# The first phase of a hybrid streaming encoder step: its loads in packed rows, the samples ahead of the prompt, and its splits placed ahead of waits

## The chip, the cores and the metric

The kernel runs on one core of one Trainium2 chip. The time is the device time of one execution in microseconds. The kernel before took 1387.94 us, the median of three runs (1385.57 to 1388.15).

Engines are named as the profile names them: PE (TensorE, matrix products) and PEld (its weight loads), DVE (VectorE), ACT (ScalarE), POOL (GpSimd) and SP (SyncE, which issues most loads). SBUF is the on-chip memory that the engines read, PSUM the one that TensorE writes.

## The reference

One layer of a mixer network, for 256 new frames (the prompt) and 32 frames of a running stream (the samples), with the same weights and a width of 2048:

```python
mod = jax.nn.silu(c) @ ada_w + ada_b                      # c: one vector per request group; ada_w 2048 x 6144
shift, scale, gate = jnp.split(mod, 3, axis=-1)
h = rms_norm(x, g_pre) * (1.0 + scale[:, None]) + shift[:, None]
proj = h @ w_in                                           # w_in 2048 x 18432
gb, gc, gu, zc, q, k, v, zr, ma, mb = jnp.split(proj, SPLIT_POINTS, axis=-1)
y_conv = gb * causal_conv3(gc * gu) * jax.nn.silu(zc)     # short convolution with a carried history
y_ret = head_rms(retention(rope(q), rope(k), v)) * jax.nn.silu(zr)   # 8 heads, carried state
merged = jax.nn.sigmoid(ma) * (y_conv @ w_branch[0]) + jax.nn.sigmoid(mb) * (y_ret @ w_branch[1])
x = x + gate[:, None] * rms_norm(merged @ w_out, g_post)
```

All is float32. Besides the new x the step returns the convolution's history and the retention's state of both groups.

## The kernel before

All products have the 288 frames (256 of the prompt, 32 samples) as columns, and run over contraction tiles of 128 rows. Float32 products are made of three faster ones: each operand is split into a high part (the value rounded to the type `F32R`) and a low part (the value less its high part), and `hi*hi`, `hi*lo` and `lo*hi` are summed in PSUM. For a weight piece, ACT makes the high part `whi` (a cast) and DVE the low part `wlo` (a subtraction); for `h` they are `hh` (ACT) and `hl` (DVE).

The change lies in the first phase (lines 210 to 441), in which four engines' work is in the order written (`manual_schedule`): each engine does its instructions strictly in the order of the code, and waits at the first that isn't ready. The phase does this:

- It loads x in three tiles (two of 128 prompt frames, one of 32 samples) on SP's queue, and eight small loads on ACT's queue bring the vectors (c, ada_b, the convolution's state and weights, norm_pre) as rows of 128 into two tiles, `crows` and `vrows`, which TensorE turns into columns (lines 380 and 382).
- `square(t)` (ACT, line 386) sums the squares of tile t; `norm(t)` (POOL takes the power, DVE scales x, line 391) normalises it; `turn_x(t)` (TensorE, line 401) transposes it in 16 pieces of 128 columns, and ACT and DVE copy these out into `xT` (line 403).
- `modulate(i)` (line 296) multiplies silu(c) with one piece of ada_w, that is 512 rows of it and, of 256 output columns, both the shift and the scale. Four pieces make one group `g`: the modulation of two contraction tiles. `gather_mod(g)` (line 306) turns the result into columns, and `factors(g)` (lines 309 to 329) makes the multiplier and the addend of each row, then, on ACT, `h` and `hh`; `low_parts(g)` makes `hl` on DVE.
- `multiply(i)` (line 339) multiplies the group's two tiles of `h` with a piece of w_in: 256 rows by 1024 columns, of q, of k or of the first half of v. It does so in four steps j of two output tiles each, 12 products a step; after a step the sums are added to `firsts` in SBUF (line 363; in group 0 they are copied, line 361). Between the steps `cut()` splits half a weight piece ahead of its use: `usual` and `rare` (line 337) say after which steps.
- There are eight groups of four ada_w pieces and three w_in pieces. The list `loads` has them in order of use, and `load(i)` issues them on SP's queue. Each piece is 1 MB and takes one of nine buffers `raw`; a load waits until the piece that had its buffer is used. `modulate` of a group stands between the `multiply` calls of the group before.

At a group's end, in its third `multiply` and ahead of step 1, stand `gather_mod` and `factors` of the next group; `cut()` follows after step 1, `low_parts` after step 2:

```python
                if nxt and j == 1:
                    gather_mod(g + 1)
                    factors(g + 1)
```

The later phases (the remaining columns of w_in, the retention, both branches and the output product) load pieces of 256 columns and split them in the same way by `product` (line 163), whose products are lines 148, 149 and 151. They aren't edited.

Of the kernel before, what the change touches and what calls it, by code (L numbers as in the profile page):

```python
# [10 lines left out]
F32 = mybir.dt.float32  # L11
F32R = mybir.dt.float32r
AF = mybir.ActivationFunctionType
ALU = mybir.AluOpType
# [77 lines left out]

@with_exitstack
def hybrid_step(ctx: ExitStack, tc, x_prompt, x_sample, c_prompt, c_sample, state_conv, state_ret,
                ada_w, ada_b, norm_pre, norm_post, w_in, conv_w, conv_b, w_branch, w_out,
                rope_t, dec_t, kdec_t, qdec_t, blk,
# [113 lines left out]
    with ExitStack() as phase:  # L210
# [14 lines left out]
        x = []  # L225
        for src in (x_prompt[0, 0:P], x_prompt[0, P:TP], x_sample[0]):
            x.append(buffer("raw", KH * WC, F32, RAW, MORE_RAW))
            nc.sync.dma_start(out=x[-1][:src.shape[0]], in_=src)


        def rows(t, r, v, n):
            A.dma_start(out=t[r * NK:(r + n) * NK], in_=v.rearrange("(k p) -> k p", p=P))

        crows = st.tile([3 * NK, P], F32, name="crows")
        rows(crows, 0, c_prompt[0], 1)
        rows(crows, 1, c_sample[0], 1)
        rows(crows, 2, ada_b[0, D:2 * D], 1)
        vrows = st.tile([NR * NK, P], F32, name="vrows")
        rows(vrows, R_SC, state_conv[0, 0].rearrange("r d -> (r d)"), 2)
        rows(vrows, R_CW, conv_w[0].rearrange("r d -> (r d)"), 3)  # L240
        rows(vrows, R_CB, conv_b[0], 1)
        rows(vrows, R_GP, norm_pre[0], 1)
        rows(vrows, R_AB, ada_b[0, 0:D], 1)
# [11 lines left out]
        def load(i):  # L255
# [3 lines left out]
            raw = buffer("raw", KH * WC, F32, RAW, MORE_RAW)  # L259
            if is_mod:  # L260
                v = raws[i] = raw.rearrange("p (k s c) -> p k s c", k=MOD, s=2)
                for s in range(2):
                    c0 = s * D + g * GS * P
                    nc.sync.dma_start(out=v[:, :, s, :], in_=ada_w[0, u * MOD * P:(u + 1) * MOD * P, c0:c0 + GS * P]
                                      .rearrange("(k p) c -> p k c", p=P))
            else:
                v = raws[i] = raw.rearrange("p (k c) -> p k c", k=GS)
                n = 1 if g == 0 and u == 0 else GS
                for k in range(0, GS, n):
                    r0 = (g * GS + k) * P  # L270
                    nc.sync.dma_start(out=v[:, k:k + n], in_=w_in[0, r0:r0 + n * P, FIRST[u]:FIRST[u] + PIECE]
                                      .rearrange("(k p) c -> p k c", p=P))
# [533 lines left out]
```

## Time and profile before

| | before |
|---|---|
| median of 3 runs | 1387.94 us |
| the profiled execution | 1388.77 us |
| its span in the profile | 1387.0 us |
| PE busy | 1348.6 us (97%) |
| DVE, ACT busy | 840.1, 552.9 us |
| mean granted clock of TensorE | 0.987 |
| read from memory | 261.75 MB |
| mean rate of the loads | 193 GB/s |

The profile tells the busy time of each engine, for the span or for any stretch of it; the clock that the throttle granted to TensorE (1 is full speed); who waited for whom; and the chain of work that ended last. A row of instructions has start and length, engine, line of the code and operation, `out<-in`, shapes, and in brackets the idle time of the engine ahead of it with what ended it. "L386 firsts<-raw" is such a name: the square's output is thrown away into a tile that isn't used yet. A DMA issue (SPq, ACTq) has the time that issuing took; its landing is told apart. Matmuls overlap, so that busy PE time counts a stretch in which products follow one another as fully busy.

### The profile page before, as it was taken

To read this page: it belongs to the slowest core of one execution; us is meant where nothing else is said; L and a number is where in the kernel's file an instruction comes from. 1 tells how busy PE (TensorE), PEld (TensorE's weight loads), DVE (VectorE), ACT (ScalarE), POOL (GpSimd) and SP (SyncE) were. 2 spreads that over 40 slices of the span, in tenths; PEclk is the share of its full clock that TensorE was granted. 3 is DMA by queue.
4 is the path that set the end of the run, shared out by engine and by line. 5 is a ranking of instruction groups with operands and counts; after the bars stand their busy time and mean duration, and the time that the engine had idled before them with its cause. 6 is when DMAs were issued, how large, how long until landed. Compare 5 with 4: busy or idle time off the path is not lost.

```text
span 1387.0 us, 24180 instructions
## 1 busy us (share of the span) xinstructions
PE 1348.6 (97%) x10250; PEld 1309.0 (94%) x10250; DVE 840.1 (61%) x1394; ACT 552.9 (40%) x824; POOL 10.0 (1%) x18
## 2 busy tenths in 40 slices
PE   4999999999999999999999999999999999999996
PEld 3888889999999999999999999999999999999996
DVE  3476768965555866666777767775555334555443
ACT  3434325754444433333334333333333333334442
POOL 0000000000000000000000000000000000000000
PEclk8999999999999999999999999999999999999998
DMA  9988864544445567566666656665455455557431
GB/s 332 371 308 302 275 225 136 166 135 161 144 147 158 182 204 217 187 214 203 199 191 202 199 185 190 213 217 182 156 165 171 153 167 167 159 175 225 158 111 69
DMA packets 240740, 267.81 MB, mean 193 GB/s; under 512 B 5604, under 2 KB 233236, under 8 KB 240020
## 3 DMA queue, kind: packets, MB, share of 16 engines
q1 hardware_dynamic: 234336, 256.13, 56.2%
q10 hardware_dynamic: 6296, 10.13, 2.9%
q8 instruction: 80, 1.31, 0.4%
q14 instruction: 28, 0.23, 0.1%
HBM read 261.75 MB, written 4.49 MB: 192 GB/s over the span
## 4 chain that ended last, share of the span: by engine, by line
issue 67%; PE 27%; DVE 3%; ACT 2%; DMA 1%; POOL 0%; DVEq 0%; POOLq 0%; ACTq 0%
PE acc L148 4%; PE acc L151 4%; PE acc L149 4%; PE pair L355 3%; PE pair L354 3%; PE pair L358 3%; PE small L296 2%; ACT h L326 1%; DVE firsts L363 1%; PE aux L476 1%; DVE wlo L284 1%; PE pair L401 1%; ACT whi L283 1%; PE aux L477 1%; PE aux L478 1%
## 5 line engine op out<-in xcount | busy, mean ns | idle before, releaser
L114 DVE TENSOR_TENSOR wlo<-raw,whi 128x1024 fp32r<-128x1024 f32 x336 | 410.6, 1222 | 348.7 <-ACT whi L113 347.9
L113 ACT CAST whi<-raw 128x1024 fp32r<-128x1024 f32 x336 | 352.6, 1050 | 516.7 <-PE acc L149 486.6
L148 PE MATMUL acc<-hh,whi 128*128 128x288 f32 x1920 | 531.4, 299 | 1.0 <-DVE firsts L363 1.0
L149 PE MATMUL acc<-hl,whi 128*128 128x288 f32 x1920 | 530.4, 297 | 0.0
L148 PEld LDWEIGHTS acc<-hh,whi 128*128 128x128 f32 x1920 | 361.0, 188 | 5.1 <-issue 1.7
L149 PEld LDWEIGHTS acc<-hl,whi 128*128 128x128 f32 x1920 | 361.2, 188 | 0.3
L151 PE MATMUL acc<-hh,wlo 128*128 128x288 f32 x1920 | 330.0, 294 | 0.0
L151 PEld LDWEIGHTS acc<-hh,wlo 128*128 128x128 f32 x1920 | 283.1, 188 | 0.0
L355 PE MATMUL pair<-hl,whi 128*128 128x288 f32 x384 | 111.1, 304 | 4.8 <-DVE hl L334 4.8
L354 PE MATMUL pair<-hh,whi 128*128 128x288 f32 x384 | 112.6, 307 | 2.8 <-ACT hh L327 2.0
L620 DVE SCALAR_TENSOR_TENSOR gbc<-raw,sc,gbc 128x256 f32<-128x256 f32 x240 | 100.3, 477 | 13.3 <-DMA raw<-in_ada_w_dram 13.3
L363 DVE TENSOR_TENSOR firsts<-pair,firsts 128x576 f32<-128x576 f32 x84 | 63.3, 754 | 41.5 <-PE pair L358 41.5
L358 PE MATMUL pair<-hh,wlo 128*128 128x288 f32 x384 | 84.2, 300 | 1.1 <-DVE wlo L284 1.1
L354 PEld LDWEIGHTS pair<-hh,whi 128*128 128x128 f32 x384 | 73.9, 192 | 11.5 <-ACT whi L283 5.7
L355 PEld LDWEIGHTS pair<-hl,whi 128*128 128x128 f32 x384 | 74.1, 193 | 6.8 <-DVE hl L334 6.4
L149 PE MATMUL acc<-ml,whi 128*128 128x288 f32 x256 | 70.6, 297 | 0.0
L148 PE MATMUL acc<-mh,whi 128*128 128x288 f32 x256 | 70.2, 296 | 0.0
L148 PE MATMUL acc<-ch,whi 128*128 128x288 f32 x256 | 70.0, 296 | 0.0
L148 PE MATMUL acc<-yh,whi 128*128 128x288 f32 x256 | 69.9, 296 | 0.0
L149 PE MATMUL acc<-yl,whi 128*128 128x288 f32 x256 | 69.8, 295 | 0.0
L149 PE MATMUL acc<-cl,whi 128*128 128x288 f32 x256 | 69.5, 294 | 0.0
L284 DVE TENSOR_TENSOR wlo<-raw,whi 128x1024 fp32r<-128x1024 f32 x48 | 58.3, 1217 | 15.3 <-ACT whi L283 15.3
(179 smaller groups left out, 1333.8 us busy)
## 6 DMA issues: line engine op xcount, KB each, us to landing
raw<-in_w_in_dram SPq DMA_DIRECT2D x143, 1024.0 KB, 5.1
raw<-in_ada_w_dram SPq DMA_DIRECT2D x64, 512.0 KB, 7.3
raw<-in_w_branch_dram SPq DMA_DIRECT2D x32, 1024.0 KB, 5.6
raw<-in_ada_w_dram SPq DMA_DIRECT2D x16, 1024.0 KB, 5.1
raw<-in_w_out_dram SPq DMA_DIRECT2D x16, 1024.0 KB, 5.5
raw<-in_x_prompt_dram SPq DMA_DIRECT2D x2, 1024.0 KB, 6.1
out_dram<-ns SPq DMA_DIRECT2D x16, 128.0 KB, 5.3
x<-in_x_prompt_dram ACTq DMA_DIRECT2D x1, 2048.0 KB, 8.0
```

Source lines behind the costliest of these rows:

```text
L113: A.copy(out=hi, in_=src)
L114: V.tensor_tensor(out=lo, in0=src, in1=hi.bitcast(F32), op=ALU.subtract)
L148: nc.tensor.matmul(ps, hi[:, k, fs], xh[:, k0 + k, :], start=first and k == 0, stop=False)
L149: nc.tensor.matmul(ps, hi[:, k, fs], xl[:, k0 + k, :], start=False, stop=False)
L151: nc.tensor.matmul(ps, lo[:, k, fs], xh[:, k0 + k, :], start=False, stop=last and k == n - 1)
L284: V.tensor_tensor(out=lo, in0=raws[i][:, k], in1=hi.bitcast(F32), op=ALU.subtract)
L296: nc.tensor.matmul(pm[at:at + 32, :GS * P], cs[:, kt, :], v[:, k, s, :], start=kt < 2, stop=kt >= NK - 2, tile_position=(0, at))
L354: nc.tensor.matmul(ps, hi[:, fs], hh[:, kt, :], start=k == 0, stop=False)
L355: nc.tensor.matmul(ps, hi[:, fs], hl[:, kt, :], start=False, stop=False)
L358: nc.tensor.matmul(ps, lo[:, fs], hh[:, kt, :], start=False, stop=k == GS - 1)
L363: V.tensor_tensor(out=sums, in0=pp[:, :, :T], in1=sums, op=ALU.add)
L620: V.scalar_tensor_tensor(out=ga[:, b], in0=raw[:, k], scalar=sc[:, kt, b:b + 1], in1=ga[:, b], op0=ALU.mult, op1=ALU.add)
```

## The change

Six things are done, all in the first phase.

- The host lays out copies of the phase's inputs (`packed`): the vectors as two tables, the pieces of ada_w and w_in each as 128 rows of 8 KB in the order of loading. Values are only moved, none is computed.
- The vectors come in two loads. They were eight.
- The loads of x stand behind these, the samples' tile first. The order of squares, norms and turns follows: samples, tile 0, tile 1. The samples are copied out by DVE alone.
- Each weight piece comes in one load of 8 KB rows, or in two halves for the pieces of ada_w of group 0 and the first of w_in. Before, a piece of ada_w was two loads of 1 KB rows, and a piece of w_in one load (the first: two) of 4 KB rows.
- `cut` is taken apart into `cut_high` (ACT) and `cut_low` (DVE). At a group's end `cut_high` stands ahead of `gather_mod`, and `low_parts` and `cut_low` follow step 1. At the start both high parts are cast by ACT, one ahead of the gather and one behind `new_h`, and both low parts stand behind `low_parts`.
- `new_h` is `factors`' second half with a name of its own. In group 0 the samples' columns of `h` and the whole second tile, with its `hh`, are made by DVE.

```diff
--- before.py
+++ after.py
@@ -90,10 +90,23 @@
     return np.ascontiguousarray(rope), d, kd, np.ascontiguousarray(qd), blk
 
 
+def packed(c_prompt, c_sample, ada_b, state_conv, conv_w, conv_b, norm_pre, ada_w, w_in):
+
+
+    rows = lambda *a: np.concatenate([np.reshape(v, (-1, P)) for v in a])
+    small = rows(c_prompt, c_sample, ada_b[0, D:2 * D])
+    table = rows(state_conv, conv_w, conv_b, norm_pre, ada_b[0, :D])
+    a = ada_w[0, :, :2 * D].reshape(NK // MOD, MOD, P, 2, NG, GS * P)
+    a = a.transpose(4, 0, 2, 1, 3, 5).reshape(NG, NK // MOD, P, MOD * 2 * GS * P)
+    w = np.stack([w_in[0, :, c:c + PIECE] for c in FIRST]).reshape(len(FIRST), NG, GS, P, PIECE)
+    w = w.transpose(1, 0, 3, 2, 4).reshape(NG, len(FIRST), P, GS * PIECE)
+    return [np.ascontiguousarray(v) for v in (small, table, a, w)]
+
+
 @with_exitstack
 def hybrid_step(ctx: ExitStack, tc, x_prompt, x_sample, c_prompt, c_sample, state_conv, state_ret,
                 ada_w, ada_b, norm_pre, norm_post, w_in, conv_w, conv_b, w_branch, w_out,
-                rope_t, dec_t, kdec_t, qdec_t, blk,
+                rope_t, dec_t, kdec_t, qdec_t, vec_small, vec_table, ada_first, w_first, blk,
                 y_prompt, y_sample, nc_prompt, nr_prompt, nc_sample, nr_sample):
     nc = tc.nc
     V, A, G = nc.vector, nc.scalar, nc.gpsimd
@@ -222,25 +235,14 @@
 
         A.preload_act_table(AF.Sigmoid)
 
-        x = []
-        for src in (x_prompt[0, 0:P], x_prompt[0, P:TP], x_sample[0]):
-            x.append(buffer("raw", KH * WC, F32, RAW, MORE_RAW))
-            nc.sync.dma_start(out=x[-1][:src.shape[0]], in_=src)
-
-
-        def rows(t, r, v, n):
-            A.dma_start(out=t[r * NK:(r + n) * NK], in_=v.rearrange("(k p) -> k p", p=P))
-
         crows = st.tile([3 * NK, P], F32, name="crows")
-        rows(crows, 0, c_prompt[0], 1)
-        rows(crows, 1, c_sample[0], 1)
-        rows(crows, 2, ada_b[0, D:2 * D], 1)
+        A.dma_start(out=crows, in_=vec_small)
         vrows = st.tile([NR * NK, P], F32, name="vrows")
-        rows(vrows, R_SC, state_conv[0, 0].rearrange("r d -> (r d)"), 2)
-        rows(vrows, R_CW, conv_w[0].rearrange("r d -> (r d)"), 3)
-        rows(vrows, R_CB, conv_b[0], 1)
-        rows(vrows, R_GP, norm_pre[0], 1)
-        rows(vrows, R_AB, ada_b[0, 0:D], 1)
+        A.dma_start(out=vrows, in_=vec_table)
+
+        x = [buffer("raw", KH * WC, F32, RAW, MORE_RAW) for _ in range(3)]
+        for t, src in ((2, x_sample[0]), (0, x_prompt[0, 0:P]), (1, x_prompt[0, P:TP])):
+            nc.sync.dma_start(out=x[t][:src.shape[0]], in_=src)
 
 
 
@@ -257,31 +259,39 @@
                 return
             is_mod, g, u = loads[i]
             raw = buffer("raw", KH * WC, F32, RAW, MORE_RAW)
+            src = (ada_first if is_mod else w_first)[g, u]
+
+            n = 2 if g == 0 and (is_mod or u == 0) else 1
+            m = KH * WC // n
+            for j in range(n):
+                nc.sync.dma_start(out=raw[:, j * m:(j + 1) * m], in_=src[:, j * m:(j + 1) * m])
             if is_mod:
-                v = raws[i] = raw.rearrange("p (k s c) -> p k s c", k=MOD, s=2)
-                for s in range(2):
-                    c0 = s * D + g * GS * P
-                    nc.sync.dma_start(out=v[:, :, s, :], in_=ada_w[0, u * MOD * P:(u + 1) * MOD * P, c0:c0 + GS * P]
-                                      .rearrange("(k p) c -> p k c", p=P))
+                raws[i] = raw.rearrange("p (k s c) -> p k s c", k=MOD, s=2)
             else:
-                v = raws[i] = raw.rearrange("p (k c) -> p k c", k=GS)
-                n = 1 if g == 0 and u == 0 else GS
-                for k in range(0, GS, n):
-                    r0 = (g * GS + k) * P
-                    nc.sync.dma_start(out=v[:, k:k + n], in_=w_in[0, r0:r0 + n * P, FIRST[u]:FIRST[u] + PIECE]
-                                      .rearrange("(k p) c -> p k c", p=P))
+                raws[i] = raw.rearrange("p (k c) -> p k c", k=GS)
 
         to_cut = [(i, k) for i, (is_mod, _, _) in enumerate(loads) if not is_mod for k in range(GS)]
 
-        def cut(cast=A.copy):
+        half_cut = []
+
+        def cut_high():
 
             if to_cut:
                 i, k = to_cut.pop(0)
                 hi = buffer("whi", PIECE, F32R, PARTS, MORE_PARTS)
+                A.copy(out=hi, in_=raws[i][:, k])
+                half_cut.append((i, k, hi))
+
+        def cut_low():
+            if half_cut:
+                i, k, hi = half_cut.pop(0)
                 lo = buffer("wlo", PIECE, F32R, PARTS, MORE_PARTS)
+                V.tensor_tensor(out=lo, in0=raws[i][:, k], in1=hi.bitcast(F32), op=ALU.subtract)
                 parts_of[i, k] = hi, lo
-                cast(out=hi, in_=raws[i][:, k])
-                V.tensor_tensor(out=lo, in0=raws[i][:, k], in1=hi.bitcast(F32), op=ALU.subtract)
+
+        def cut():
+            cut_high()
+            cut_low()
 
         def modulate(i):
 
@@ -318,15 +328,23 @@
             V.tensor_tensor(out=mul, in0=mod[:, :, 1, :], in1=each(ab1[:, ks]), op=ALU.add)
             V.tensor_tensor(out=mul, in0=mul, in1=each(vecs[:, R_GP, ks]), op=ALU.mult)
             V.tensor_tensor(out=add, in0=mod[:, :, 0, :], in1=each(vecs[:, R_AB, ks]), op=ALU.add)
-            hs = []
+            state_of[g] = mul, add
+
+        def new_h(g):
+            mul, add = state_of[g]
+            state_of[g] = hs = []
             for f in range(GS):
                 h = st.tile([P, T], F32, name="h", tag="h", bufs=GS)
-                xt = xT[:, g * GS + f, :]
+                kt = g * GS + f
+                on_v = g == 0 and f == 1
                 for b, c in enumerate((slice(0, TP), slice(TP, T))):
-                    A.activation(h[:, c], xt[:, c], AF.Identity, scale=mul[:, f, b:b + 1], bias=add[:, f, b:b + 1])
-                A.copy(out=hh[:, g * GS + f, :], in_=h)
+                    if on_v or (g == 0 and b):
+                        V.tensor_scalar(out=h[:, c], in0=xT[:, kt, c], scalar1=mul[:, f, b:b + 1],
+                                        scalar2=add[:, f, b:b + 1], op0=ALU.mult, op1=ALU.add)
+                    else:
+                        A.activation(h[:, c], xT[:, kt, c], AF.Identity, scale=mul[:, f, b:b + 1], bias=add[:, f, b:b + 1])
+                (V.tensor_copy if on_v else A.copy)(out=hh[:, kt, :], in_=h)
                 hs.append(h)
-            state_of[g] = hs
 
         def low_parts(g):
             for f, h in enumerate(state_of.pop(g)):
@@ -344,8 +362,10 @@
             nxt = u == NU - 1 and g + 1 < NG
             for j in range(NF // 2):
                 if nxt and j == 1:
+                    cut_high()
                     gather_mod(g + 1)
                     factors(g + 1)
+                    new_h(g + 1)
                 pp = pair_tile()
                 for f in range(2):
                     ps, fs = pp[:, f, :T], slice((2 * j + f) * P, (2 * j + f + 1) * P)
@@ -361,9 +381,10 @@
                     (V.tensor_copy if j % 2 else A.copy)(out=sums, in_=pp[:, :, :T])
                 else:
                     V.tensor_tensor(out=sums, in0=pp[:, :, :T], in1=sums, op=ALU.add)
-                if nxt and j == 2:
+                if nxt and j == 1:
                     low_parts(g + 1)
-                for _ in range(cuts.get(j, 0)):
+                    cut_low()
+                for _ in range(cuts.get(j, 0) - (nxt and j == 1)):
                     cut()
 
 
@@ -400,37 +421,39 @@
                 for k in range(m):
                     nc.tensor.transpose(out=pp[:, k * n:(k + 1) * n], in_=x[t][:n, (k0 + k) * P:(k0 + k + 1) * P],
                                         identity=ident[:n, :n])
-                (V.tensor_copy if k0 else A.copy)(out=xT[:, k0:k0 + m, t * P:t * P + n],
+                (V.tensor_copy if k0 or t == 2 else A.copy)(out=xT[:, k0:k0 + m, t * P:t * P + n],
                                                   in_=pp[:, :m * n].rearrange("p (k n) -> p k n", k=m))
 
-        square(0)
+        square(2)
         cv = vp[:, :2 * NK].rearrange("p (b k) -> p k b", b=2)
         sg = st.tile([P, NK, 2], F32, name="sg")
         A.activation(sg, cv, AF.Sigmoid)
+        square(0)
+        square(1)
+        norm(2)
         V.tensor_tensor(out=sc, in0=cv, in1=sg, op=ALU.mult)
         V.tensor_copy(cs[:, :, 0:2], sc)
         ab1 = st.tile([P, NK], F32, name="ab1")
         V.tensor_scalar(out=ab1, in0=vp[:, 2 * NK:3 * NK], scalar1=1.0, scalar2=None, op0=ALU.add)
+        V.tensor_copy(vecs, vp2[:, :NR * NK].rearrange("p (r k) -> p r k", r=NR))
         norm(0)
-        square(1)
-        V.tensor_copy(vecs, vp2[:, :NR * NK].rearrange("p (r k) -> p r k", r=NR))
+        turn_x(2)
+        norm(1)
         turn_x(0)
         modulate(0)
-        square(2)
-        norm(1)
         turn_x(1)
-        modulate(1)
-        norm(2)
-        turn_x(2)
         for i in range(NBUF - len(x), NBUF - 1):
             load(i)
-        modulate(2)
-        modulate(3)
+        for i in range(1, NK // MOD):
+            modulate(i)
+        cut_high()
         gather_mod(0)
         factors(0)
-        cut(V.tensor_copy)
+        new_h(0)
+        cut_high()
         low_parts(0)
-        cut()
+        cut_low()
+        cut_low()
 
         for i, (is_mod, g, u) in enumerate(loads):
             load(i + NBUF - 1)
@@ -792,6 +815,9 @@
     *consts, blk = tables()
     named = [(n, np.ascontiguousarray(inputs[n])) for n in _INS]
     named += list(zip(["rope_t", "dec_t", "kdec_t", "qdec_t"], consts))
+    named += list(zip(["vec_small", "vec_table", "ada_first", "w_first"],
+                      packed(*(inputs[n] for n in ("c_prompt", "c_sample", "ada_b", "state_conv", "conv_w", "conv_b",
+                                                   "norm_pre", "ada_w", "w_in")))))
     for name, a in named:
         arrays[f"in_{name}_dram"] = a
         args.append(nc.dram_tensor(f"in_{name}_dram", a.shape, mybir.dt.from_np(a.dtype), kind="ExternalInput").ap())
```

## The prediction

> **What bounds the kernel now.** I read the page first, then busy time by stretch, then what TensorE waited for, then the chain of waits through the first 40 us, and last the timeline around the start and one group boundary.
>
> ```profile
> span 1387.0 us, 24180 instructions
> ```
>
> ```profile
> 0.00:240.00 240.00, 214.62 (x1776) 189.09 (x1777) 144.88 (x213) 91.47 (x134) 2.38 (x9) 0.95 0.82 281
> 240.00:1387.00 1147.00, 1133.94 (x8477) 1119.93 (x8475) 695.24 (x1182) 461.38 (x691) 7.67 (x9) 1.00 0.55 175
> ```
>
> The columns of the two stretches are length, busy time of PE, PEld, DVE, ACT and POOL, then granted clock, DMA share and GB/s. Behind 240 us TensorE is busy for 1133.9 of 1147 us at full clock, with the DMA engines at 0.55 of theirs. The stretch ahead of 240 us, which alone is edited, holds 25 us without TensorE work and has a mean clock of 0.95. The later stretch is TensorE's own, so an earlier start of it should move the end one to one.
>
> Where the first stretch loses time, first by what TensorE waited for (total, times, longest), then by the chain (start, length):
>
> ```profile
> PE pair L401 <- DVE raw L391: 5.7, 3, 2.5
> PE pair L355 <- DVE hl L334: 4.8, 7, 1.8
> ...
> PE pair L358 <- DVE wlo L284: 1.1, 3, 0.5
> ```
>
> ```profile
> 0.74 4.85 DMA raw<-in_x_prompt_dram
> 5.61 3.29 DMA vrows<-in_norm_pre_dram
> ...
> 9.79 1.30 DVE raw L391
> 11.13 3.35 PE pair L401 x16
> ...
> 16.47 1.30 DVE raw L391
> ...
> 23.27 1.29 DVE raw L391
> ...
> 26.57 3.62 PE small L296 x32
> ...
> 37.12 0.61 PE pair L358
> ```
>
> Three rounds of normalise (DVE, L391) and turn (PE, L401) follow one another from 9.8, 16.5 and 23.3 us, and the last modulation products (L296) stand behind the third. Only at 37.1 us has TensorE all that its first weight piece needs, the last `wlo` (L358). The weights' transfers did not hold it: none of these rows names ada_w. Two waits of SP's queue say why the first round is late:
>
> ```profile
> SPq L228 <- DMA crows<-in_c_sample_dram: 4.9, 1, 4.9
> ...
> SPq L264 <- DMA vrows<-in_state_conv_dram: 0.7, 1, 0.7
> ```
>
> In order of issue c_sample is the third load and x_sample the eleventh; state_conv is the fifth and the second half of the first ada_w piece the thirteenth. A load waits for the load eight places ahead. The eight small vector loads, slow beside the 1 MB loads of x, thus hold SP back, and ACT too: norm_pre, ninth, is issued at 5.61, when the first load has landed (0.74 + 4.85).
>
> **The change, part by part: the start.** I rebuild these 37 us from durations of before. Two rows give the time of a load to landing, two a transfer rate (last column), the rest lengths on the engines:
>
> ```profile
> raw<-in_x_sample_dram SPq DMA_DIRECT2D x1, 256.0 KB, 3.4
> ...
> crows<-in_c_prompt_dram ACTq DMA_DIRECT2D x1, 8.0 KB, 2.9
> ```
>
> ```profile
> 6.00:8.00 2.00, 0.31 (x1) 0.18 (x1) 0.00 (x0) 1.55 (x1) 0.00 (x0) 1.00 1.19 421
> ...
> 16.00:18.00 2.00, 0.19 (x1) 0.20 (x2) 1.29 (x1) 0.04 (x1) 0.43 (x1) 0.85 1.09 348
> ```
>
> ```profile
> 6.45 1.91 ACT L386 ACTIVATE firsts<-raw 128x2048 f32<-128x2048 f32 x1 [4.43 <-DMA raw<-in_x_prompt_dram]
> ...
> 10.99 0.28 DVE L416 COPY vecs<-small 128x128 f32<-128x128 f32 x1
> ...
> 14.40 1.07 PE L296 MATMUL small<-raw,cs 128*32 128x256 f32 x16
> ...
> 15.64 0.14 DVE L189 TENSOR_SCALAR ms<-ss 128x1 f32<-128x1 f32 x1
> ...
> 30.64 1.01 PE L306 MATMUL small<-pick,modrow 128*128 128x4 f32 x4 [0.49 <-ACT modrow L300]
> ...
> 32.22 0.90 ACT L326 ACTIVATE h<-xT,add,mul 128x256 f32<-128x256 f32 x2 [1.63 <-DVE add L320]
> ...
> 33.63 0.29 PEld L354 LDWEIGHTS pair<-hh,whi 128*128 128x128 f32 x1 [2.07 <-ACT hh L327]
> ```
>
> Two vector loads in place of eight free ACT's queue six loads earlier, and the first SP load to wait for one eight places ahead is then the fourth half-load of ada_w, which waits for a vector load. x_sample goes out at 0.74 and lands after 2.9 to 3.4 us: I take 4.1. Its 256 KB push the first x_prompt load from 5.59 to about 6.25 (0.26 MB at 0.4 MB per us). ACT squares the samples by 6.2 (1.91 and a read of 0.2), does the sigmoid (0.2), and squares the two prompt tiles by 9.0 and 11.2. From the end of a square to the scaled x is 0.83 (15.64 to 16.47) plus 1.29. So DVE has the samples scaled at 8.4, spends some 0.8 on four small operations that were there before (the longest, L416, takes 0.28), has tile 0 at 9.2 + 2.1 = 11.3, then the samples' copy out (0.6, an estimate: half of a tile's length) and tile 1 at 14.1. TensorE turns the samples inside the wait, tile 0 from 11.5 to 14.9 (3.35), multiplies the first modulation piece (1.07) to 16.0, turns tile 1 to 19.4, and does the other three pieces (3 x 1.07) by 22.6. They have landed: the last x at about 9.1, the 4.19 MB of ada_w behind it 10 us later at 421 GB/s, 12 at 348, so by 19 to 21, and the first half of w_in at 21 to 22.6.
>
> Then the row is copied (0.4), gathered and made into factors (1.58 from 30.64 to 32.22), and the first `h` and `hh` made, 1.41 before (32.22 to 33.63), about 1.1 now, since DVE takes the 32 sample columns. The first product starts at 25.7 against 33.6. DVE then does two `hl` (0.45 each) and two `wlo` (1.23 each, L284): the last `wlo` is read at about 29.2 against 37.1. `cut_high` ahead of the gather costs ACT 1.05 while it would wait for TensorE; without that cover the cast returns to the path for 1.05. **The start gives 8 us.** Bounds: a late table of vectors keeps the sigmoid, and with it both squares, back by 1.0; the three products at half clock, as in the row of 26.57 (3.62 for two pieces), add 2.2; a sample landing at 3.6 gives 0.5, a gather at full clock 0.5. So 5 to 9.
>
> **The group boundaries.** One of them, DVE and ACT in order of time:
>
> ```profile
> 83.57 0.90 ACT L326 ACTIVATE h<-xT,add,mul 128x256 f32<-128x256 f32 x2 [2.51 <-DVE add L320]
> ...
> 85.78 0.43 ACT L327 CAST hh<-h 128x288 fp32r<-128x288 f32 x1
> ...
> 86.12 3.88 ACT L283 CAST whi<-raw 128x1024 fp32r<-128x1024 f32 x4
> ...
> 87.20 1.23 DVE L284 TENSOR_TENSOR wlo<-raw,whi 128x1024 fp32r<-128x1024 f32 x1 [1.97 <-ACT whi L283]
> ...
> 88.34 0.75 DVE L363 TENSOR_TENSOR firsts<-pair,firsts 128x576 f32<-128x576 f32 x1
> ...
> 89.01 0.82 DVE L334 TENSOR_TENSOR hl<-h,hh 128x288 fp32r<-128x288 f32 x2
> ...
> 89.51 0.40 PE L355 MATMUL pair<-hl,whi 128*128 128x288 f32 x1 [0.59 <-DVE hl L334]
> ```
>
> DVE idles 1.97 until ACT has cast `whi`, and `hl` stands behind that `wlo` and a sum. In the new order ACT casts ahead of `h`, in an idle time of 2.51. DVE finishes the second `hl` at 86.2 + 0.45 = 86.7 and `wlo` at 87.9; the sum of j=2 follows at 87.9, where it ran at 88.34. TensorE arrives at 88.5 and needs this `wlo` 0.7 later: the wait is gone, and what is next to be late, `wlo`, has 1.3 to spare. Six boundaries wait thus, and the longest is followed by half clock:
>
> ```profile
> PE pair L355 <- DVE hl L334: 4.6, 6, 1.8
> ```
>
> ```profile
> 212.50:214.30 1.80, 0.02 (x1) 0.03 (x1) 1.80 (x4) 1.80 (x3) 0.00 (x0) 1.00 0.01 2
> 215.30:218.80 3.50, 3.50 (x18) 3.50 (x17) 1.85 (x2) 0.00 (x0) 0.00 (x0) 0.51 0.70 240
> ```
>
> The 3.5 us at 0.51 hold 1.7 us of loss, which the 1.8 us hole ahead of them brought. 4.6 + 1.7, and some 0.2 at the boundary out of group 0, where two splits stand behind one another: **6.5 us**, 4 if `wlo` comes late at some boundaries, 7 at most. The Trainium skill (TensorE: Matmul & The Clock Gate, Part 1) puts the halving behind an idle window of about 3.4 us and calls half clock the default state. By that rule the 1.8 us hole would not have sufficed, and the boundaries would give 4.8; here the dip follows the hole directly, so I go by the rows.
>
> **The loads** themselves: rows of 8 KB in one transfer for two save SP's issuing and raise the rate, 421 against 348 in the rows above. I cost this at nothing, because TensorE's work hides it: none of its waits above names a weight load. One group of before is this stretch:
>
> ```profile
> 113.40:138.30 24.90, 24.31 (x217) 21.41 (x213) 16.55 (x24) 8.74 (x14) 0.00 (x0) 1.00 0.90 310
> ```
>
> When TensorE starts 8 us earlier and a group takes 0.6 less, it wants seven pieces of 1.05 MB in 24.3 us, 302 GB/s, which either rate carries. SP still refills x's buffers when x is turned, now at 14.9 and 19.4 us, with data queued until about 24, so the DMA engines do not run dry. `cut_high` on ACT adds a wait for the next group's raw piece, with `h` and `hh` queued behind it and TensorE behind them; as the pieces run several loads ahead, I put it at nothing, at 1 us for a piece 3 us late.
>
> **Sum:** 8 + 6.5 = 14.5. The profiled execution took 1388.77 (its span of 1387.0 and 1.77 around it), so 1374.3; it lay 0.83 over the median of the runs, 1387.94, so the forecast is 1373.5. The bounds of both parts, 9 to 16 us of gain, make 1372 to 1379, and the three runs before spread over 2.6.
>
> **The rivals.** *Half clock at the start.* The row of 26.57 shows products at half speed after holes of 2 to 3 us; the new order leaves no hole from 11.5 to 22.6, which speaks against it. If it happens, +2.2 there and about 1.3 in the gather and the first products: 1377. *The wait changes its name.* If DVE reaches `wlo` 1.3 us later than I work out, TensorE waits for it in place of `hl` at all boundaries, and only the start is won: 1380. For it: DVE is in strict order and the sum of j=1 lies ahead. *Nothing arrives*, because the start is held by transfers after all: to cost the start its 8 us, the last ada_w piece would land at 29.5, 4.19 MB in 20.4 us or 205 GB/s, against 348 in the slower row above. Then the new order only moves the idle time about, and the boundaries follow the transfers: 1387. *Slower: contiguous 1 MB pieces are slow to read.* The phase's products end now with this row:
>
> ```profile
> 234.66 0.43 PE L358 MATMUL pair<-hh,wlo 128*128 128x288 f32 x2
> ```
>
> It moves 56 weight pieces and x, 61.1 MB. The last piece's splits and 48 products take 8.7, so it must land by 226, and the rival decides below 61.1 / 224, 272 GB/s. At 265 it lands at 233 and the products end at 241.5: 1394. Against it: the x tiles have this very form and moved at 421.
>
> **How the numbers follow.** Forecast 0.66, half clock 0.14, renamed wait 0.09, nothing 0.05, slower 0.06. A measurement of this kernel tells 0.2%, 2.8 us, from no change; the first three lie over it: faster 0.89, same 0.05, slower 0.06. The range takes in the bounds and the first two rivals, 1367 to 1382; below it lies what exceeds both upper bounds.
>
> **What would show it.** In the changed profile: x_sample landed before 4.2; no SP wait for a vector load over 1 us; the three rounds from 7, 10 and 13 us; the last first-piece `wlo` product near 29; no wait of L355-like products for `hl` beyond the first, and no stretch at half clock near 200 us; the 1147 us behind the phase unchanged. The prediction is wrong if TensorE's waits name `raw` loads, if `wlo` takes the place of `hl`, or if the later stretch grows by what the first one loses.

## The result, and the profile after

The changed kernel takes 1370.60 us, the median of four runs (1369.78 to 1370.98), against 1386.76 for the kernel before beside it (four runs, 1384.25 to 1388.15). The ratio is 0.9885, with a 95% interval of 0.9868 to 0.9902. Run once more, beside three of the experiments and on their chip, it took 1370.71 (1370.44 to 1370.84) against 1387.86. So it is 16 to 17 us faster; 14.5 were forecast.

The profiled execution took 1370.98 us. Its page begins:

```profile
span 1369.2 us, 24142 instructions
## 1 busy us (share of the span) xinstructions
PE 1342.6 (98%) x10250; PEld 1306.0 (95%) x10250; DVE 841.7 (61%) x1398; ACT 552.2 (40%) x820; POOL 10.0 (1%) x18
```

The span is 17.8 us shorter. Where that lies is read from the first product of the next phase. The timeline of the kernel before has it at 236.05:

```profile
236.05 0.37 PE L148 MATMUL acc<-hh,whi 128*128 128x288 f32 x1 [0.95 <-DVE firsts L363]
```

The timeline of the changed kernel has it at 217.49:

```profile
217.49 0.37 PE L161 MATMUL acc<-hh,whi 128*128 128x288 f32 x1 [0.96 <-DVE firsts L383]
```

The first phase has become 18.6 us shorter. What follows, where nothing was edited, was 1150.95 us and is 1151.7.

What TensorE waited for in the changed kernel (total, times, longest):

```profile
PE pair L374 <- ACT hh L346: 1.7, 1, 1.7
PE pair L378 <- DVE wlo L289: 1.6, 3, 0.7
PE pair L422 <- DVE raw L412: 1.5, 2, 0.8
```

No product waits for `hl` any more (4.8 us before), and turns wait for normalised x for 1.5 us in place of 5.7. The chain of waits through the start (start, length):

```profile
0.74 3.52 DMA raw<-in_x_sample_dram
...
7.21 1.27 DVE raw L412
...
9.87 1.30 DVE raw L412
11.22 3.67 PE pair L422 x16
14.89 1.40 PE small L306 x16
16.29 1.90 PE pair L422 x16
18.19 2.77 PE small L306 x48
...
24.51 2.28 DVE wlo L289 x2
26.83 0.61 PE pair L378
```

The last `wlo` of the first piece is used at 26.83, 10.3 us earlier than before. Between the two tiles' turns there is a difference to note: the first takes 3.67 us, the second 1.90, for the same 16 transposes. Behind 26.83 some of the gain is given back, as the busy time by stretch shows (the clock is the third number from the end of a row):

```profile
26.00:28.00 2.00, 1.30 (x6) 1.17 (x6) 0.78 (x1) 0.00 (x0) 0.00 (x0) 0.50 1.02 426
28.00:30.00 2.00, 2.00 (x10) 2.00 (x10) 0.00 (x0) 0.64 (x1) 0.00 (x0) 0.50 0.98 406
30.00:32.00 2.00, 2.00 (x10) 2.00 (x9) 0.20 (x1) 0.86 (x1) 0.00 (x0) 0.50 1.03 430
```

TensorE works at half clock until 32.7. The next modulation products start at 35.35 where they started at 44.92, so 9.6 of the 10.3 us arrive.

TensorE's rows say where these 10.3 lie. The turn of tile 0 starts at 11.2 in both kernels (11.13 and 11.22), and the modulation products end at 30.15 before and at 20.92 now: 9.2 are gained by then, and what follows them (gather, factors, `h`, the casts and splits) adds 1.1. Between 11.2 and the end of the modulation, TensorE waited 4.8 us for normalised x (2.3 and 2.5 in two waits) and now waits for nothing; the samples' turn of 1.9 has gone into a wait; tile 1's turn and the modulation products take 3.0 less (1.90 in place of 3.42, and 4.2 in place of 5.6), since they run largely at full clock; tile 0's turn takes 0.3 more.

A group boundary, the one that the prediction showed, now reads in the timeline:

```profile
70.83 1.05 ACT L282 CAST whi<-raw 128x1024 fp32r<-128x1024 f32 x1
...
73.45 0.91 ACT L345 ACTIVATE h<-xT,add,mul 128x256 f32<-128x256 f32 x2 [1.56 <-DVE add L330]
...
76.12 0.46 DVE L352 TENSOR_TENSOR hl<-h,hh 128x288 fp32r<-128x288 f32 x1 [0.66 <-ACT hh L346]
76.50 1.22 DVE L289 TENSOR_TENSOR wlo<-raw,whi 128x1024 fp32r<-128x1024 f32 x1
77.39 1.07 PE L306 MATMUL small<-raw,cs 128*32 128x256 f32 x16
77.64 1.42 DVE L383 TENSOR_TENSOR firsts<-pair,firsts 128x576 f32<-128x576 f32 x2
```

The cast stands in ACT's idle time, `hl` and `wlo` are done at 76.6 and 77.7, and TensorE, at its modulation products until 78.4, finds both ready. From the first modulation product behind group 0 (62.85 before, 53.28 after) to the end of the phase it was 173.2 us and is 164.2: the boundaries gave 9.0. Taken from one start of modulation products to the next, the last boundary gave 3.7 of this (2.0 of its hole and 1.7 of the half clock behind it), the five in the middle 0.76 to 1.08 each, 0.91 in the mean, and the one out of group 0 gave 0.56.

### The profile page after: what moved, and what is told of

It is laid out like the page before. It is cut to its first block, busy times and chain, and to the rows that moved or that the text cites. A ratio compares the mean times of both kernels' runs of the same rounds, so it can differ in the third digit from the quotient of the medians.

```text
span 1369.2 us, 24142 instructions
## 1 busy us (share of the span) xinstructions
PE 1342.6 (98%) x10250; PEld 1306.0 (95%) x10250; DVE 841.7 (61%) x1398; ACT 552.2 (40%) x820; POOL 10.0 (1%) x18
## 4 chain that ended last, share of the span: by engine, by line
issue 68%; PE 30%; DVE 1%; DMA 0%; ACT 0%; POOL 0%; DVEq 0%; POOLq 0%; ACTq 0%
PE acc L161 4%; PE pair L374 4%; PE acc L162 4%; PE acc L164 4%; PE pair L378 4%; PE pair L375 4%; PE small L306 2%; PE aux L499 1%; PE aux L500 1%; PE aux L501 1%; PE aux L604 0%; PE pair L422 0%; DVE wlo L289 0%; DVE x L798 0%; DMA raw<-in_x_sample_dram 0%
## 5 line engine op out<-in xcount | busy, mean ns | idle before, releaser
L127 DVE TENSOR_TENSOR wlo<-raw,whi 128x1024 fp32r<-128x1024 f32 x336 | 411.2, 1224 | 347.8 <-ACT whi L126 347.0
L643 DVE SCALAR_TENSOR_TENSOR gbc<-raw,sc,gbc 128x256 f32<-128x256 f32 x240 | 100.7, 484 | 14.5 <-DMA raw<-in_ada_w_dram 14.4
L374 PEld LDWEIGHTS pair<-hh,whi 128*128 128x128 f32 x384 | 73.4, 191 | 10.3 <-ACT whi L282 4.8
L378 PEld LDWEIGHTS pair<-hh,wlo 128*128 128x128 f32 x384 | 62.9, 191 | 2.5 <-DVE wlo L289 2.3
```

The lines of the kernel that those rows point to most:

```text
L127: V.tensor_tensor(out=lo, in0=src, in1=hi.bitcast(F32), op=ALU.subtract)
L374: nc.tensor.matmul(ps, hi[:, fs], hh[:, kt, :], start=k == 0, stop=False)
L378: nc.tensor.matmul(ps, lo[:, fs], hh[:, kt, :], start=False, stop=k == GS - 1)
L643: V.scalar_tensor_tensor(out=ga[:, b], in0=raw[:, k], scalar=sc[:, kt, b:b + 1], in1=ga[:, b], op0=ALU.mult, op1=ALU.add)
```

## The experiments

The theory from the first two profiles: there are two independent gains, the start and the boundaries, and each boundary wait cost more than its row says. Every kernel ran four or five times, beside the kernel before and on the same chip. The first four kernels share one chip (before: 1387.79); the changed kernel's 1370.60 was not taken there.

**The start alone.** The boundaries are put back:

```diff
                 if nxt and j == 1:
-                    cut_high()
                     gather_mod(g + 1)
...
-                if nxt and j == 1:
+                if nxt and j == 2:
                     low_parts(g + 1)
-                    cut_low()
-                for _ in range(cuts.get(j, 0) - (nxt and j == 1)):
+                for _ in range(cuts.get(j, 0)):
```

> The changed kernel with the group boundaries in the old order (low_parts after step 2, cut after step 1, no cut_high ahead of the gather). Everything at the start and the packed rows stay. Theory A (two independent gains, each wait priced by the spacing of the products around it in the two traces): the start gives 9.6, the boundaries about 8, so 1377. Theory B (prediction's sizes, waits priced as the rows of TensorE's waits give them): the boundaries are worth 6.5 and this run is about 8 under the kernel before, 1378 to 1379 if the start is 8. Rival C (the waits at the boundaries vanish because the pieces arrive earlier, whatever the order): no wait for hl left and 1371.

Measured: 1377.22 (1376.71 to 1379.07), ratio 0.9926 (0.9914 to 0.9939): 10.6 us under the kernel before, 6.5 to 6.6 over the changed one's two medians, as theory A has it. TensorE's waits have the old row again:

```profile
PE pair L374 <- DVE hl L352: 4.6, 6, 1.8
```

So earlier pieces do not remove these waits; the order does, and rival C falls. In this profile the long hole of 1.8 us is there, at 202, but half clock does not follow it:

```profile
202.00:204.00 2.00, 0.27 (x3) 0.03 (x1) 2.00 (x4) 2.00 (x3) 0.00 (x0) 1.00 0.00 0
204.00:206.00 2.00, 1.93 (x14) 1.86 (x15) 2.00 (x4) 0.56 (x1) 0.00 (x0) 1.00 0.89 305
```

Of the five runs two, at 1378.7 and 1379.1, have a mean clock of 0.992 to 0.993, the others, at 1376.7 to 1377.2, 0.994. A dip of about 1.7 us in some executions and not in others would do that; the runs without a profile do not show where it lies.

Why the same hole is followed by half clock in one profile and not in the other, the traces' clock records let one guess. In each profile the changes of the clock lie whole multiples of 3.41 us apart, as if it were set anew in steps of that length. In the kernel before the hole lies whole within the step from 211.96 to 215.37, in which TensorE was busy for 1.62 us. Here, counted on from the change at 31.72, a step begins at 202.39, just behind the start of the hole at 202.27, and TensorE was busy for 1.73 us of it. So it may be chance how much of a hole falls into one step. A limit can't be read from this: with the idle turns below, a step with 1.79 us busy was followed by half clock.

**The boundaries alone**, put into the kernel before by the same lines, with `cut` taken apart as in the change:

```diff
                 if nxt and j == 1:
+                    cut_high()
                     gather_mod(g + 1)
...
-                if nxt and j == 2:
+                if nxt and j == 1:
                     low_parts(g + 1)
+                    cut_low()
-                for _ in range(cuts.get(j, 0)):
+                for _ in range(cuts.get(j, 0) - (nxt and j == 1)):
```

> The kernel before with only the boundary's new order (cut_high ahead of gather_mod, low_parts and cut_low after step 1). Theory A: each of five middle boundaries gives 0.95 (spacing of products in the traces), the last 3.5 with its stretch at half clock, the one out of group 0 0.5: 8 to 9 us under the kernel before. Theory B: 6.5 under. Rival C: 0 to 2 under, and waits for wlo in place of hl. Under A and B no product waits for hl behind the first piece, and no stretch at half clock near 215 us.

Measured: 1379.57 (1376.17 to 1380.48), ratio 0.9934 (0.992 to 0.9949): 8.2 under, as theory A has it, and no stretch at half clock is left near 215 us. Its waits:

```profile
PE pair L370 <- DVE wlo L290: 0.6, 2, 0.4
...
PE pair L367 <- DVE hl L345: 0.2, 1, 0.2
```

The 0.2 for `hl` is the first piece's. Nothing took the place of the waits. The two parts, 10.6 and 8.2, make 18.8; the changed kernel's 1370.60 lies 17.2 under this kernel before. So they add to within the spread of the kernel before, which alone is 3.9 us. The half clock behind the last boundary can count twice in the sum: the start alone is without it in some runs by chance, the boundaries alone by their order.

**The rows of 8 KB.** The pieces are read from the original arrays:

```diff
-            src = (ada_first if is_mod else w_first)[g, u]
...
+                for s in range(2):
+                    c0 = s * D + g * GS * P
+                    nc.sync.dma_start(out=v[:, :, s, :], in_=ada_w[0, u * MOD * P:(u + 1) * MOD * P, c0:c0 + GS * P]
+                                      .rearrange("(k p) c -> p k c", p=P))
...
```

> The changed kernel with the weight pieces of the first phase read from the original arrays again (ada_w in two loads of 1 KB rows a piece, w_in in 4 KB rows). Theory A (the prediction: the layout is worth nothing, TensorE hides it): 1370.6, within 0.5. Rival D (with the start so much shorter, the transfers are what comes last): at 350 GB/s instead of 409 the fourth ada_w piece lands at about 21.5 against 19.2, after TensorE would want it at 20, and the w_in halves at 23 to 24: the first products start 1.5 to 2.5 later, 1372 to 1373, and a modulation product or a cast waits for ada_w or w_in in the trace.

Measured: 1372.15 (1371.08 to 1372.64), ratio 0.9885 (0.9871 to 0.9898). TensorE's waits and the timeline of this kernel:

```profile
PE small L309 <- DMA raw<-in_ada_w_dram: 0.6, 1, 0.6
```

```profile
21.44 1.06 PE L309 MATMUL small<-raw,cs 128*32 128x256 f32 x14 [0.63 <-DMA raw<-in_ada_w_dram]
...
25.28 0.40 PE L377 MATMUL pair<-hh,whi 128*128 128x288 f32 x1 [1.68 <-ACT hh L349]
```

The transfers are last here, and the first product starts at 25.28 against 23.70; rival D has both this and the time. How much of it reaches the end needed a run beside the changed kernel on one chip (changed there: 1370.71):

> The weight pieces from the original arrays once more, now beside the changed kernel. Theory D (the first run showed a modulation product waiting 0.6 for ada_w and the first products at 25.3 instead of 23.7): 1.2 to 1.8 slower than the changed kernel in this call. Rival (the first difference was one between chips): within 0.5.

Measured: 1371.21 (1371.00 to 1371.85), 0.5 over the changed kernel, with the first product at 25.24 against 23.50 there. Theory D's time missed. The 0.5 is the edge of what its rival allowed, but the rival's reason fails: beside the changed kernel, too, the start is 1.7 later. Part of it comes back, for the next modulation products start at 35.86 against 35.05; the half clock lasts 6.8 us in both profiles and here falls in part on TensorE's waits. The four runs of each do not overlap, so the layout seems to be worth half a microsecond, 0.04%, at the end.

**The vectors' loads.** Eight small loads in place of two:

```diff
-        A.dma_start(out=crows, in_=vec_small)
+        rows(crows, 0, c_prompt[0], 1)
...
-        A.dma_start(out=vrows, in_=vec_table)
+        rows(vrows, R_SC, state_conv[0, 0].rearrange("r d -> (r d)"), 2)
...
```

> The changed kernel with the eight small vector loads in place of the two tables; the order of x and all else as changed. Theory A (a load waits for the load eight places ahead): norm_pre, ninth in order, waits for the samples' load and holds ACT's first square back by about 0.9; the second prompt tile, eleventh, waits for c_sample until about 6.5; ada_w lands some 2 us later; start 1.5 to 2.5 later, 1372 to 1373. Rival E (the vectors' number does not matter once x's loads stand with the samples first): 1370.6.

Measured: 1372.57 (1372.17 to 1373.10), ratio 0.9889 (0.9875 to 0.9902); 1.9 over the changed kernel, though not on one chip. Its timeline:

```profile
4.01 0.32 ACTq L239 DMA_DIRECT2D vrows<-in_norm_pre_dram  x1
...
4.85 1.91 ACT L416 ACTIVATE firsts<-raw 32x2048 f32<-32x2048 f32 x1 [2.84 <-DMA crows<-in_c_prompt_dram]
...
22.89 0.64 PE L315 MATMUL small<-raw,cs 128*32 128x256 f32 x8 [0.64 <-DMA raw<-in_ada_first_dram]
```

norm_pre is held until the samples have landed and holds ACT's first square back by 0.5 (4.35 in the changed kernel), less than the 0.9 expected; ada_w, held in its turn, then makes the last modulation products wait, and they end near 23.5 where they ended at 21. Theory A holds; of the 2.5 by which the modulation ends later, the first square has 0.5 and the waits for ada_w 1.3.

**The order of x** taken back to tile 0, tile 1, samples (this kernel and the next three share a second chip; before: 1388.98):

```diff
-        for t, src in ((2, x_sample[0]), (0, x_prompt[0, 0:P]), (1, x_prompt[0, P:TP])):
+        for t, src in ((0, x_prompt[0, 0:P]), (1, x_prompt[0, P:TP]), (2, x_sample[0])):
...
-        square(2)
+        square(0)
...
+        turn_x(2)
...
```

> The changed kernel with the order of x taken back: loads, squares, norms and turns go tile 0, tile 1, samples; all else as changed. Theory A (it is the number of early loads and their waits that counted, not which tile comes first, since the sample tile costs ACT 1.91 and DVE 1.27 like a full one): tile 0 is turned from about 10 instead of 11.2, the samples' turn comes onto TensorE's path behind it for 1 to 1.9, and the modulation ends at the same 21: 1370.6 within 0.7. Rival F (samples first is what shortens the start, as their turn hides in a wait): 1.5 to 2.5 slower, 1372 to 1373.

Measured: 1369.91 (1369.65 to 1370.13), ratio 0.9864 (0.9851 to 0.9878). Beside the changed kernel on one chip:

> The order of x taken back once more, now beside the changed kernel. Theory A (the sample tile's place is worth nothing): within 0.7 of the changed kernel in this call, if anything faster. Rival F: 1.5 to 2.5 slower.

Measured: 1369.85 (1369.70 to 1370.37) against 1370.71. The samples' earlier place gains nothing; the old order is 0.9 us better, and the four runs of each do not overlap. The timeline of the first of these runs says why it costs nothing:

```profile
10.19 3.60 PE L422 MATMUL pair<-ident,raw 128*128 128x128 f32 x16
...
14.73 1.97 PE L422 MATMUL pair<-ident,raw 128*128 128x128 f32 x16
...
17.27 1.14 PE L422 MATMUL pair<-ident,raw 32*128 32x32 f32 x16 [0.58 <-DVE raw L412]
18.34 2.90 PE L306 MATMUL small<-raw,cs 128*32 128x256 f32 x48
```

Tile 0 is turned 1.0 earlier, the samples' turn costs 1.14 and a wait of 0.58 ahead of it, and the last products start within 0.2 us of where they did.

**The slow first turn.** TensorE is kept busy ahead of 11 us by 36 transposes of the identity that nobody reads:

```diff
+        idle_turns(13)
         vp = small_tile()
...
+        idle_turns(14)
         vp2 = small_tile()
...
+        idle_turns(3)
...
         turn_x(2)
+        idle_turns(6)
         norm(1)
```

> The changed kernel with 36 extra transposes of the identity into a spare PSUM tile on TensorE, in its waits ahead of 11 us; their output is read by nobody. In the changed profile the first full tile is turned in 3.67 us and the second in 1.97, both under a recorded clock of 1.00. Theory G (TensorE begins at half clock and the record does not show it before the first change): kept busy, it turns tile 0 in about 2.0 and the modulation behind it takes 1.0 and not 1.47, so the products start 1 to 2 earlier until the transfers (ada_w's last half lands near 19) are last: 1369 to 1369.6. Rival H (the record is right and the first turn is slow for another reason, PSUM or SBUF): tile 0 still takes 3.67 and the time is 1370.6 or a little more.

Measured: 1370.73 (1369.82 to 1371.84), ratio 0.9871 (0.9857 to 0.9884). The timeline:

```profile
1.36 3.03 PE L404 MATMUL pair<-ident 128*128 128x128 f32 x13 [1.36 <-POOL ident masks.py:199]
...
11.22 1.97 PE L431 MATMUL pair<-ident,raw 128*128 128x128 f32 x16 [0.70 <-DVE raw L421]
...
19.67 0.64 PE L306 MATMUL small<-raw,cs 128*32 128x256 f32 x8 [1.72 <-DMA raw<-in_ada_first_dram]
...
20.94 0.64 PE L306 MATMUL small<-raw,cs 128*32 128x256 f32 x8 [0.64 <-DMA raw<-in_ada_first_dram]
```

The turn of tile 0 falls from 3.67 to 1.97 us, though the recorded clock is 1.00 in both: theory G's mechanism holds and H's falls. The trace says why the record misses it. Its first clock record begins at 5.51, in the changed kernel at 15.69, and ahead of the first record a view reads 1.00. The idle transposes start 0.21 apart up to 5.4 and 0.11 apart from 5.6 on.

The time does not follow, not even by the 1 us expected, and is the one that H gave. TensorE reaches the last two modulation halves 2 us sooner, waits 2.4 us for their data, and is done with them at 21.58, no sooner than the changed kernel at 20.92. So the transfers stand right behind TensorE at the start. And behind the wait half clock comes earlier, from 22.58 to 32.82, where it lasted from 25.93 to 32.75.

**The high parts first.** In the first piece, six output tiles get all products with `whi`, then all with `wlo`; a tile's sum is the same:

```diff
+                ahead = [pair_tile() for _ in range(3)]
+                outs = [(pp[:, f, :T], slice((2 * j + f) * P, (2 * j + f + 1) * P)) for j, pp in enumerate(ahead) for f in range(2)]
+                for k, (hi, lo) in enumerate(parts):
+                    for src in (hh, hl):
+                        for ps, fs in outs:
+                            nc.tensor.matmul(ps, hi[:, fs], src[:, k, :], start=k == 0 and src is hh, stop=False)
+                for k, (hi, lo) in enumerate(parts):
+                    for ps, fs in outs:
+                        nc.tensor.matmul(ps, lo[:, fs], hh[:, k, :], start=False, stop=k == GS - 1)
```

> The changed kernel with the first weight piece's products in another order: for the first six output tiles all products with the high parts of the weights, then all with the low parts; the sums are the same. Theory I (what the start still loses behind 23.7 us is waiting for wlo, 1.2, and the half clock that these holes bring, 26 to 32.7): the six tiles' 36 products end near 28.5 and the piece near 30.5 instead of 35; the next w_in piece lands at about 31, so its products can start at 33 to 34 instead of 37.2: 3 less, 1367.5. Rival J (transfers come next and take most of it back): a cast waits longer for w_in and 1369.5 to 1370.6.

Measured: 1367.70 (1367.50 to 1369.21), ratio 0.9851 (0.9838 to 0.9865), 2.9 us under the changed kernel's 1370.60, which was not taken on this chip. On one chip with it ran the old order of x alone (1369.91): 2.2 under that. By stretch:

```profile
24.00:27.00 3.00, 3.00 (x23) 3.00 (x24) 3.00 (x4) 0.86 (x1) 0.00 (x0) 1.00 1.01 423
27.00:33.00 6.00, 5.80 (x61) 4.48 (x60) 1.55 (x3) 2.47 (x4) 0.00 (x0) 1.00 1.01 422
```

TensorE has work while DVE makes `wlo`, and the half clock is gone. What is waited for next is the next w_in piece, by its cast:

```profile
31.17 1.05 ACT L282 CAST whi<-raw 128x1024 fp32r<-128x1024 f32 x1 [2.03 <-DMA raw<-in_w_first_dram]
```

It has the lowest median of all kernels here, and theory I's 1367.5 came.

**Both, and the second piece loaded earlier.** The idle turns, 12 more behind the first gather, the high parts first, and

```diff
-            loads += (w[:1] + m[:1] if g == 0 else m[:1] + w[:1]) + m[1:2] + w[1:2] + m[2:] + w[2:]
+            loads += w[:2] + m + w[2:] if g == 0 else m[:1] + w[:1] + m[1:2] + w[1:2] + m[2:] + w[2:]
```

> The idle turns and the high parts first together, 12 more idle turns behind the first gather, and in group 0 the second w_in piece loaded and used ahead of the next group's ada_w pieces. Theory I+G: the second piece lands near 26 and its products follow the first piece's at about 30, the third piece's start near 41 instead of 45.6: 4 to 5 less than the changed kernel, 1366. Rival J: the transfers are last whatever the order, 1369 to 1370.

Measured: 1369.32 (1367.14 to 1369.72), ratio 0.9857 (0.9844 to 0.987). The profiled run is the one at 1367.14; the other three lie over 1369 at a clock of 0.993 to 0.994 where it has 0.995. It is not better than the high parts first alone; the 1366 missed, and the time is the one of rival J. What the three slower runs lost can't be read from the one profile.

**The old order of x with the high parts first** (beside the changed kernel on one chip):

> The order of x taken back, and the first weight piece's products with all high parts ahead of the low parts. Theory I: 2.5 to 3.5 faster than the changed kernel in this call, 1367 to 1368, as the high parts first alone, because the next w_in piece lands at about 31 in either order of x. Rival: the two do not add and it is 1369.5 to 1370.5.

Measured: 1368.05 (1367.97 to 1368.26), ratio 0.9858 (0.9843 to 0.9873), 2.7 under the changed kernel, as expected, and no gain over the high parts first alone. Against the old order of x alone, which ran beside it (1369.85), the high parts first give 1.8.

## Why the prediction was right, step by step

**The bound and the sum's form** held. The later phases took 1150.9 to 1151.7 us in every profile here, so an earlier end of the first phase moved the end by nearly all of it. The sizes held less well: both parts came out above their upper bounds (10.3 against 9 at the start, 9.0 against 7 at the boundaries, both by the profiles), and the time lies below the 1372 that these bounds made. That the range reached down to 1367 is what took it in.

**The start** was forecast at 8 us with 9 as its bound, to the last `wlo`: 10.3, of which 9.6 reached the next modulation products. The walk held to 0.3 us up to the turn of tile 0. That this ended at 14.9 as forecast is luck in part: it started 0.3 sooner and took 0.3 longer. Then the walk missed at the turn of tile 1, for which 3.35 was taken and 1.90 measured, at the products behind it (2.8 against 3.2), and at the gather (0.62 against 1.03). The step that failed is the price of a turn: the row of 3.35 stood in a stretch with a granted clock of 1.00, and I took it as the price at full clock. The idle turns showed that it is the price at half clock. The profile of before has a hint of it, in two stretches that a turn fills (the clock is again the third number from the end):

```profile
12.00:14.00 2.00, 2.00 (x12) 2.00 (x11) 0.00 (x0) 0.86 (x1) 0.00 (x0) 1.00 1.05 339
18.00:20.00 2.00, 2.00 (x11) 2.00 (x11) 0.00 (x0) 0.19 (x1) 0.00 (x0) 0.50 1.09 348
```

The same turn runs no faster under 1.00 than under 0.50, and the first clock record of that trace begins only at 13.98. The other direction was missed too: a half-clock stretch behind 26 us, which took 0.7 back.

**The causes at the start.** That a load waits for the load eight places ahead, and that the vectors held the rest back, is borne out (1.9 us with eight loads again). The samples' earlier place, which the walk began with, is worth nothing. These two and the layout explain less than half of the 9.6. By TensorE's rows, what follows the modulation, with the casts and DVE's share of `h`, has 1.1 of the 10.3; ahead of it the gain is waits for normalised x that are gone, and the half clock that went with them, which points to the new order of squares, norms and turns. No run changed that order alone, so this part is read from rows and not shown by an experiment.

**The boundaries** were forecast at 6.5: 6.5 by the start-alone kernel's distance to the changed one, 8.2 put into the kernel before, 9.0 between the two profiles. The profile of the start alone has no half clock at its end, and its boundaries take 7.3 more than the changed kernel's. Two terms were mis-sized and point in opposite directions. Each middle wait was priced at its row's 0.59, but in the timeline before, the product that waited started 0.99 behind its forerunner where 0.13 is usual; the row counts idle time only from the modelled end of the product ahead, which is 0.27 later than the next could have started. That boundary so cost 0.86, and the five gave 0.91 in the mean. And the half clock behind the last boundary, 1.7 us, I ascribed to the 1.8 us hole ahead of it as if it always came. The start-alone kernel has the same hole without it. The Trainium skill (TensorE: Matmul & The Clock Gate, Part 1) calls the window in which activity is counted free-running, and that agrees with a hole that is sometimes followed by half clock and sometimes not.

**The loads** were costed at nothing, since TensorE's work would hide them. One of the signs to look for did not come: SP waited 2.2 us for a vector load (the table), where none was to wait over 1 us, though no wait of TensorE in the changed kernel names a weight load. At the start TensorE's cover is thinner than I said: with the old rows the first product comes 1.6 to 1.7 us later and a modulation product waits for ada_w. It ends at 0.5 us. The rate was right: 397 to 436 GB/s from 4 to 26 us.

**The rivals.** Half clock at the start came, but not where I placed it: the first turn ran so, and then the first products behind the gather; the three modulation pieces that I had priced ran at full clock. The wait did not change its name, the later phases did not give the gain back, and contiguous pieces were not slow. With 1370.6 the time lies between my forecast, 1373.5, and the lower end, 1367.

## What to carry to other kernels

Price a wait at a boundary by the spacing of the starts around it, not by its idle row: behind a product that ends late the row left out 0.27 us of what the wait cost here. Before a duration is carried to another place, look at how the same instruction runs elsewhere in the trace; two lengths under one recorded clock, or one length under two, mean that the record does not tell the whole state. And where two operands become ready one behind the other, do first the work that needs only the first: it gave 1.8 to 2.9 us here with no instruction more.

## What the runs showed of the hardware

TensorE began at half speed while the profile gave its clock as 1.00: 16 transposes took 3.67 us from 11 us on, 1.97 from 16 us on, and 1.97 from 11 us on when it had been kept busy since 1.4 us. Those idle transposes started 0.21 us apart up to 5.4 us and 0.11 apart from 5.6 us on, and the first clock record of that trace begins at 5.51. In the first phase the stretches at half clock lasted 3.41, 6.83, 10.24 or 17.07 us, whole multiples of 3.41. A hole of 1.8 us was followed by 3.41 us of half clock in one profile, and by none in another. With one core at work, 8 KB rows came in at 397 to 436 GB/s over 20 us.
